# A four-layer decoder trunk on one core: tensor-engine operands that begin at eight different 32-byte offsets within 256 bytes

## The chip, the core and the metric

The kernel runs on one core of one Trainium2 chip. The metric is the device time of one execution in microseconds (us), taken as the median of several runs. Lower is better.

## The reference

The reference is a decoder trunk of four layers over one residual stream of 256 tokens by 1024 features, all in float32. Each layer is a token mixer followed by a squared-ReLU MLP of width 4096. Layers 0 and 3 mix by differential attention, layer 1 by block attention (with 256 tokens there is one block, so it is causal attention), layer 2 by a sliding window of 128 with sinks. Cut to what matters:

```python
for i in range(DEPTH):                       # 4
    a = rms_norm(h, attn_norm_g[i])
    y = mixer(i % 3)(a, w_in, w_out, ...)    # diff, moba, swa, diff
    h = h + y
    a = rms_norm(h, mlp_norm_g[i])
    u = jnp.maximum(a @ w_up[i], 0)          # 1024 -> 4096
    h = h + (u * u) @ w_down[i]              # 4096 -> 1024
return rms_norm(h, final_norm_g)
```

## The kernel before, in words

The residual stream is held transposed in SBUF: features on the 128 partitions, 256 tokens along the free axis, in four tiles `hT`. All weights are streamed once from HBM as pieces of 128 partitions by 2048 floats (8 KB a partition) into `raw` tiles, of which there are four.

Each product keeps near-float32 accuracy by splitting both operands into a rounded part and the rest, both of type float32r ("hi" and "lo"), and adding hi·hi, hi·lo and lo·hi. `stage` (L71 to L82) makes the two parts of each weight piece: ScalarE copies `raw` into `whi` (L80), VectorE writes the difference into `wlo` (L81), three buffers of each. `norm_part` (L220 to L227) makes the two parts of the normalized stream in four tiles `hg`, and `up_proj` (L648 to L668) those of the MLP's hidden activations, `uu`, in the slots below. `take` (L86) hands the next piece to the stage that wants it and keeps the pieces ahead fetched and split.

TensorE's work is a long row of matmuls, each with its own weight load of 128 by 128. In the MLP a `block_step` (L590) issues a pair: the hi weights against the hi and lo parts of the activations side by side (512 moving columns, L591), and the lo weights against the hi part alone (256 columns, L592). The first projections of the mixers (`proj`, L273) and the last down-projection (`down_out`, L679) issue triples, with the weight piece as the moving operand, of 512 columns and in the sliding-window layer of 256; the scores (`scores`, L311) and the differential layers' output projection (`out_proj_all`, L615) issue triples too, through `mm3` (L267).

All that is neither streamed nor constant lives in one SBUF pool, `sb`. Its large tiles share slots by number: `room(j, ...)` (L52) gives a tile in slot j, 0 to 17, and every tile that was in that slot before must be done first. A slot is 4096 bytes a partition. The names in it: `uu` in the MLP; `qk`, `qhl`, `kpadh`, `kpadl`, `v`, `e`, `et`, `oo` in the mixers.

The order of instructions on each engine is set by a scheduler when the program is built: it takes the program order and the tiles' buffers and lets an instruction go ahead when its operands and its buffer are free in its own model. `junk` (L396) is a tile with one buffer into which ScalarE writes squares that nobody reads; only their sums (`ss`) are used, in the differential layers (`diff_pair`, L389).

Of the kernel before, what the change touches and what calls it, by code (L numbers as in the profile page):

```python
# [11 lines left out]
F32 = mybir.dt.float32  # L12
F32R = mybir.dt.float32r
# [5 lines left out]
P = 128  # L19
D = 1024  # L20
S = 256
# [7 lines left out]
LOOK = 2  # L29
FAR = 5  # L30
WARM = 12
RAW = 4


def f(ap):
    return ap.bitcast(F32)
# [3 lines left out]
def trunk(ctx: ExitStack, tc: tile.TileContext, xT, gains, lams, swa_row, fng, weights, out):  # L40
# [5 lines left out]
    sb = ctx.enter_context(tc.tile_pool(name="sb", bufs=2))  # L46
    ps = ctx.enter_context(tc.tile_pool(name="ps", bufs=4, space=bass.MemoryType.PSUM))

    def bank(tag, name):
        return ps.tile([P, 512], F32, tag=tag, name=name, bufs=4)  # L50

    def room(j, shape, name, dt=F32):  # L52

        return sb.tile(shape, dt, tag=f"slot{j}", name=name, bufs=1)


    fetched, staged = [], []
# [1 line left out]
    def fetch(parts=1, first=None):  # L59

        i = len(fetched)
        raw = sb.tile([P, 2048], F32, tag="raw", name=f"raw{i}", bufs=RAW)
        w = 2048 // parts
# [7 lines left out]
    def stage(w=1024, first=None):  # L71
        i = len(staged)
        raw = fetched[i]
        hi = sb.tile([P, 2048], F32R, tag="whi", name=f"whi{i}", bufs=LOOK + 1)
        lo = sb.tile([P, 2048], F32R, tag="wlo", name=f"wlo{i}", bufs=LOOK + 1)
        for h in range(2048 // w):
            if first:
                first()
            s = slice(h * w, (h + 1) * w)
            A.activation(hi[:, s], raw[:, s], AF.Copy)  # L80
            V.tensor_tensor(lo[:, s], raw[:, s], f(hi[:, s]), op=OP.subtract)  # L81
        staged.append((hi, lo))  # L82
# [3 lines left out]
    def take():  # L86
        i = used[0]
        used[0] += 1
        while len(fetched) < min(weights.shape[0], i + FAR + 1):
            fetch()  # L90
        while len(staged) < min(weights.shape[0], i + LOOK + 1):
            stage()
        return staged[i]

    def r3(n):
        return lambda t: t.rearrange("p (a b) -> p a b", a=n)
# [43 lines left out]
    def bcast(dram, n):  # L140
        return bass.AP(tensor=dram.tensor, offset=dram.offset, ap=[[0, P], [1, n]])
# [46 lines left out]
    def lambdas():  # L188
        lam_init = [0.8 - 0.6 * math.exp(-0.3 * i) for i in (0, 3)]
        lv = room(4, [P, 4, 2, HD], "lv")  # L190
        nc.sync.dma_start(lv, bcast(lams, 8 * HD))
        lp = sb.tile([P, 2, 2, HD], F32, tag="ropea", name="lp")
        V.tensor_tensor(lp, lv[:, 0::2], lv[:, 1::2], op=OP.mult)
        ls = cst.tile([P, 2, 2], F32, name="ls")
        V.tensor_reduce(ls, lp, axis=AX.X, op=OP.add)
        A.activation(ls, ls, AF.Exp)
        V.tensor_tensor(nlam, ls[:, 1], ls[:, 0], op=OP.subtract)
        for s in range(2):
            V.tensor_scalar(nlam[:, s:s + 1], nlam[:, s:s + 1], -lam_init[s], None, op0=OP.add)
            V.tensor_scalar(sg[:, s:s + 1], sg[:, s:s + 1], 1.0 - lam_init[s], None, op0=OP.mult)  # L200

    def rsqrt(y, x, n):

        t = tiny.tile([P, n], F32, tag="nw", name="nw", bufs=6)
        V.tensor_scalar(y.bitcast(I32), x.bitcast(I32), -0.5, 1597463007.0, op0=OP.mult, op1=OP.add)
        for _ in range(3):
            V.tensor_tensor(t, y, y, op=OP.mult)
            V.scalar_tensor_tensor(t, t, -0.5, x, op0=OP.mult, op1=OP.mult)
            V.scalar_tensor_tensor(y, t, 1.5, y, op0=OP.add, op1=OP.mult)
# [5 lines left out]
    def new_norm(gain):  # L215
        n = Normed()
        n.gain, n.both, n.acc = gain, [], None
        return n

    def norm_part(n, d):  # L220

        j, b = d // 2, d % 2
        if b == 0:
            n.both.append(sb.tile([P, 2, 2, S], F32R, tag=f"hg{j}", name=f"hg{j}", bufs=1))
        both, h, g = n.both[j][:, b], hT[j][:, S * b:S * b + S], n.gain[:, d:d + 1]
        A.activation(both[:, 0], h, AF.Copy, scale=g)  # L226
        V.scalar_tensor_tensor(both[:, 1], h, g, f(both[:, 0]), op0=OP.mult, op1=OP.subtract)  # L227
# [83 lines left out]
    def scores(q, k, mask, sinks):  # L311
# [8 lines left out]
        out = []  # L320
        scored[0] += 1
        pair_e = room(4 + scored[0] % 2, [P, 2, 3 * P], "e")
        for c in range(2):
            ns = sb.tile([P, 3 * P], F32, tag="ns", name="ns", bufs=2)
# [18 lines left out]
    def transposed(es):  # L343
        turned[0] += 1
        ts = room((6, 7, 12, 13)[turned[0] % 4], [P, 2, 3 * P], "et")
        for i, e in enumerate(es):
            p = bank("wk", "p_t")
            for j in range(3):
                T.transpose(p[:, P * j:P * j + P], e[:, P * j:P * j + P], ident)  # L349
            A.activation(ts[:, i], p[:, :3 * P], AF.Copy)  # L350
        return [ts[:, i] for i in range(len(es))]

    def times_v(o, et, v):

        T.matmul(o(0), et[:, 0:P], v(0), start=True, stop=True)
        T.matmul(o(1), et[:, P:2 * P], v(0), start=True, stop=False)
        T.matmul(o(1), et[:, 2 * P:3 * P], v(1), start=False, stop=True)
# [9 lines left out]
    def part(b, n=1):  # L367

        if b % 2 == 0:
            pair[:] = [room(14 + b // 2, [P, 2, 2, S], "oo", F32R)]  # L370
        return pair[0] if n == 2 else pair[0][:, b % 2]
# [17 lines left out]
    def diff_pair(slot, ets, v, el, b):  # L389

        p = bank("wk", "p_av")
        for c in range(2):
            times_v(lambda t, c=c: p[:, S * c + P * t:S * c + P * t + P], ets[c], v[c])
        ss = tiny.tile([P, 2 * NT], F32, tag="ss", name="ss")
        for t in range(2 * NT):
            junk = sb.tile([P, P], F32, tag="junk", name="junk", bufs=1)  # L396
            A.activation(junk, p[:, P * t:P * t + P], AF.Square, accum_out=ss[:, t:t + 1])
        V.scalar_tensor_tensor(ss, ss, 1.0 / P, el, op0=OP.mult, op1=OP.add)
        y = tiny.tile([P, 2 * NT], F32, tag="ry", name="ry")
        rsqrt(y, ss, 2 * NT)  # L400
        o = sb.tile([P, 2 * NT, P], F32, tag="o", name="o")
        V.tensor_tensor(o, p.rearrange("p (t m) -> p t m", m=P), y[:, :, None].to_broadcast([P, 2 * NT, P]),
                        op=OP.mult)
        yield
        p = bank("wk", "p_o")
        for t in range(2 * NT):
            T.transpose(p[:, P * t:P * t + P], o[:, t, :], ident)
        both, gain = part(b, 2), sg[:, slot:slot + 1]
        A.activation(both[:, :, 0], r3(2)(p), AF.Copy, scale=gain)
        V.scalar_tensor_tensor(both[:, :, 1], r3(2)(p), gain, f(both[:, :, 0]), op0=OP.mult, op1=OP.subtract)  # L410
        yield [both[:, 0], both[:, 1]]
# [61 lines left out]
    def mixer_layer(i, n):  # L473
# [46 lines left out]
        else:  # L520
# [25 lines left out]
            def AV(h):  # L546
                if mixer:
                    next(heads[h], None)
                elif h % 2:
                    pairs[h // 2] = diff_pair(slot, [ets[h - 1], ets[h]], [vh(h - 1), vh(h)], els[h // 2], h - 1)  # L550
                    next(pairs[h // 2])
# [48 lines left out]
    def into(n, d, p, row, whole=False):  # L600

        j, b = d // 2, d % 2
        h = hT[j][:, S * b:S * b + S]
        y = p
        if not whole:
            y = sb.tile([P, S], F32, tag="y", name="y")
            joined(y, p)
        if row is not None:
            V.tensor_tensor(y, y, row, op=OP.mult)
        V.tensor_tensor(h, y, h, op=OP.add)  # L610
        norm_part(n, d)
        if b:
            norm_sum(n, j)
# [65 lines left out]
    def down_out(us, res, factor):  # L679

        grow = sb.tile([P, D], F32, tag="raw", name="grow", bufs=RAW)
        nc.sync.dma_start(grow, bcast(fng, D))
# [31 lines left out]
    n = new_norm(gv[:, 0, 0, :])  # L714
    blocks = iter(range(8))
    for _ in range(2):
        stage(512, lambda: norm_part(n, next(blocks)))
    for j in range(4):
        norm_sum(n, j)
    for i in range(DEPTH):  # L720
        parts = mixer_layer(i, n)
        n = new_norm(gv[:, 1, i, :])
# [24 lines left out]
        if i + 1 < DEPTH:  # L747
            n = new_norm(gv[:, 0, i + 1, :])
# [80 lines left out]
```

## Time and profile before

| what | value |
|---|---|
| median of the runs shown | 1160.81 us (1160.3, 1160.81, 1161.35) |
| profiled execution, first to last instruction (span) | 1158.7 us |
| TensorE matmuls in the trace | 6484, busy 1140.8 us |
| TensorE weight loads, busy | 980.9 us |
| VectorE, busy | 832.8 us |
| ScalarE, busy | 663.7 us |
| HBM traffic | 197 MB, 171 GB/s over the span |

The profiled execution's own time is its span, 1158.7 us; the timed runs lie about 2.1 us above it, which is what stands before the first and after the last instruction and the spread of the runs. Busy time of TensorE counts matmuls whose ends are modelled and that overlap one another, so it says little of how fast they follow each other. That is read from the starts of matmuls in a long row: the time between two of them, divided by the matmuls between.

### The profile page before, as it was taken

The numbers are of one execution on the slowest core, as the hardware profiler recorded it, in microseconds if no ns is written. First come the engines' busy times: TensorE is split into PE (matmuls) and PEld (weight loads), VectorE is DVE, ScalarE is ACT, GpSimd is POOL, SyncE is SP. The second block draws the span as 40 slices with busy tenths as digits, with TensorE's granted clock in tenths as the row PEclk, the third lists the DMA queues.
The fourth block names the chain that finished last, engine by engine and source line by source line (L and its number), as shares of the span: only waits on it lengthen the run. The fifth ranks groups of instructions, "written<-read, shape, count | busy, mean of one in ns | idle before, by whom it ended". The sixth has DMA issues, their size and how long they took to land.

```text
span 1158.7 us, 16976 instructions
## 1 busy us (share of the span) xinstructions
PE 1140.8 (98%) x6484; PEld 980.9 (85%) x6484; DVE 832.8 (72%) x1672; ACT 663.7 (57%) x1213; POOL 11.4 (1%) x39
## 2 busy tenths in 40 slices
PE   9999999999999999999999999999999999999996
PEld 7788888888887788888899688888888889888885
DVE  7887977656676697775669798775567788777453
ACT  6876656544476666654446665654447676655341
POOL 1000000000000000000000000000000000000000
PEclk9999999999999999999999999999999999999998
DMA  9543465555544355555553245555553444554540
GB/s 330 188 145 111 164 203 193 200 185 184 180 146 146 114 178 202 199 182 186 190 213 127 73 146 190 199 193 182 185 198 132 153 151 141 194 194 163 194 169 37
DMA packets 30321, 198.66 MB, mean 171 GB/s; under 512 B 3488, under 2 KB 4640, under 8 KB 7072
## 3 DMA queue, kind: packets, MB, share of 16 engines
q1 hardware_dynamic: 29952, 197.06, 49.3%
q8 instruction: 51, 0.84, 0.3%
q10 hardware_dynamic: 288, 0.52, 0.1%
q14 instruction: 30, 0.25, 0.1%
HBM read 196.52 MB, written 1.05 MB: 171 GB/s over the span
## 4 chain that ended last, share of the span: by engine, by line
PE 89%; DVE 6%; ACT 2%; DMA 1%; issue 1%; SPq 0%; ACTq 0%
PE p_up L591 20%; PE p_in L294 15%; PE p_down L591 15%; PE p_up L592 10%; PE p_down L592 8%; PE p_last L270 2%; PE p_last L269 2%; PE p_last L271 2%; DVE wlo L81 2%; PE p_e L591 1%; PE p_t L349 1%; PE p_d L591 1%; PE p_s L269 1%; DMA raw<-in_weights 1%; PE p_av L429 1%
## 5 line engine op out<-in xcount | busy, mean ns | idle before, releaser
L81 DVE TENSOR_TENSOR wlo<-raw,whi 128x1024 fp32r<-128x1024 f32 (+1 forms) x374 | 447.3, 1209 | 203.3 <-ACT whi L80 202.8
L80 ACT ACTIVATE whi<-raw 128x1024 fp32r<-128x1024 f32 (+1 forms) x374 | 384.2, 1045 | 211.9 <-issue 109.8
L591 PE MATMUL p_up<-hg,whi 128*128 128x512 f32 x1024 | 356.8, 393 | 0.2
L592 PE MATMUL p_up<-hg,wlo 128*128 128x256 f32 x1024 | 285.2, 279 | 0.0
L591 PE MATMUL p_down<-uu,whi 128*128 128x512 f32 x768 | 266.4, 392 | 0.0
L591 PEld LDWEIGHTS p_up<-hg,whi 128*128 128x128 f32 x1024 | 191.6, 187 | 43.3 <-DVE hg L227 0.7
L592 PE MATMUL p_down<-uu,wlo 128*128 128x256 f32 x768 | 214.3, 279 | 0.0
L294 PE MATMUL p_in<-whi,hg 128*128 128x512 f32 (+1 forms) x736 | 212.5, 371 | 0.3 <-ACT whi L80 0.2
L592 PEld LDWEIGHTS p_up<-hg,wlo 128*128 128x128 f32 x1024 | 193.2, 189 | 0.4
L591 PEld LDWEIGHTS p_down<-uu,whi 128*128 128x128 f32 x768 | 143.7, 187 | 32.2
L294 PEld LDWEIGHTS p_in<-whi,hg 128*128 128x128 f32 x736 | 132.1, 188 | 23.5 <-ACT whi L80 1.3
L592 PEld LDWEIGHTS p_down<-uu,wlo 128*128 128x128 f32 x768 | 144.8, 188 | 0.0
L294 PE MATMUL p_in<-wlo,hg 128*128 128x512 f32 (+1 forms) x368 | 129.9, 368 | 0.2 <-DVE wlo L81 0.2
L664 ACT ACTIVATE uu<-u 128x512 fp32r<-128x512 f32 x64 | 40.5, 633 | 72.2 <-DVE u L662 72.2
L294 PEld LDWEIGHTS p_in<-wlo,hg 128*128 128x128 f32 x368 | 68.8, 189 | 11.7 <-DVE wlo L81 0.8
L597 ACT ACTIVATE cross<-p_up 128x256 f32<-128x256 f32 x128 | 48.2, 376 | 39.6 <-PE p_up L592 34.8
L226 ACT ACTIVATE hg<-hT,gn 128x256 fp32r<-128x256 f32 x64 | 31.7, 502 | 66.4 <-DVE hT L610 65.0
L334 ACT ACTIVATE e<-ns,nm 128x128 f32<-128x128 f32 (+1 forms) x128 | 56.9, 446 | 11.0 <-DVE nm L331 10.3
L665 DVE TENSOR_TENSOR uu<-u,uu 128x512 fp32r<-128x512 f32 x64 | 44.2, 691 | 21.8 <-ACT uu L664 21.8
L598 DVE TENSOR_TENSOR relu<-p_up,cross 128x256 f32<-128x256 f32 x128 | 53.5, 418 | 1.4 <-ACT cross L597 1.3
L271 PE MATMUL p_last<-whi,uu 128*128 128x512 f32 x128 | 49.8, 389 | 0.0
L270 PE MATMUL p_last<-wlo,uu 128*128 128x512 f32 x128 | 49.8, 389 | 0.0
(181 smaller groups left out, 1245.1 us busy)
## 6 DMA issues: line engine op xcount, KB each, us to landing
raw<-in_weights SPq DMA_DIRECT2D x181, 1024.0 KB, 4.9
raw<-in_weights SPq DMA_DIRECT2D x8, 256.0 KB, 4.5
raw<-in_weights SPq DMA_DIRECT2D x4, 512.0 KB, 8.1
hT<-in_xT SPq DMA_DIRECT2D x8, 128.0 KB, 4.3
bias<-in_swa_row SPq DMA_DIRECT2D x1, 512.0 KB, 3.5
grow<-in_fng SPq DMA_DIRECT2D x1, 512.0 KB, 3.7
out<-res ACTq DMA_DIRECT2D x2, 256.0 KB, 2.7
out<-res SPq DMA_DIRECT2D x2, 256.0 KB, 2.7
```

The source lines that it names most:

```text
L80: A.activation(hi[:, s], raw[:, s], AF.Copy)
L81: V.tensor_tensor(lo[:, s], raw[:, s], f(hi[:, s]), op=OP.subtract)
L270: T.matmul(out, lh, rl, start=False, stop=False, **kw)
L271: T.matmul(out, ll, rh, start=False, stop=stop, **kw)
L294: T.matmul(out[t], n.both[k // 2][:, k % 2, x, P * t:P * t + P], r3(kb)(parts[k // kb][w])[:, k % kb, :], start=fresh, stop=k == 7 and x + ...
L334: A.activation(e[:, s], ns[:, s], AF.Exp, bias=nm[:, t:t + 1], scale=-1.0, accum_out=l[:, t:t + 1])
L591: T.matmul(r3(2)(p), hi, x, start=start, stop=False, skip_group_check=True)
L592: T.matmul(p[:, :S], lo, x[:, 0], start=False, stop=stop, skip_group_check=True)
L597: A.activation(cross, p[:, S:], AF.Copy)
L598: V.tensor_tensor(out, p[:, :S], cross, op=OP.add)
L664: A.activation(both[:, :, 0], r3(2)(u), AF.Copy)
L665: V.tensor_tensor(both[:, :, 1], r3(2)(u), f(both[:, :, 0]), op=OP.subtract)
```

## The change

The tiles that TensorE reads get 8 floats (32 bytes) more than they need, and only the first part of each is used. Since the pool places tile behind tile, each buffer then begins 32 bytes further on, modulo 256, than the one before it. This is done for the buffers of `whi` and `wlo`, the four `hg` and the slots 0 to 12; the slots 13 to 17 stay at 4096 bytes. To make room, `junk` gives up its own 512 bytes and takes a buffer of `y`, a tile with two buffers.

```diff
+STEP = 8
...
     def room(j, shape, name, dt=F32):
-        return sb.tile(shape, dt, tag=f"slot{j}", name=name, bufs=1)
+        n = math.prod(shape[1:])
+        t = sb.tile([P, 1024 + STEP * (j < 13)], dt, tag=f"slot{j}", name=name, bufs=1)[:, :n]
+        if len(shape) == 2:
+            return t
+        axes = "abcd"[:len(shape) - 1]
+        return t.rearrange(f"p ({' '.join(axes)}) -> p {' '.join(axes)}",
+                           **{a: k for a, k in zip(axes[1:], shape[2:])})
...
-        hi = sb.tile([P, 2048], F32R, tag="whi", name=f"whi{i}", bufs=LOOK + 1)
-        lo = sb.tile([P, 2048], F32R, tag="wlo", name=f"wlo{i}", bufs=LOOK + 1)
+        hi = sb.tile([P, 2048 + STEP], F32R, tag="whi", name=f"whi{i}", bufs=LOOK + 1)[:, :2048]
+        lo = sb.tile([P, 2048 + STEP], F32R, tag="wlo", name=f"wlo{i}", bufs=LOOK + 1)[:, :2048]
...
-            n.both.append(sb.tile([P, 2, 2, S], F32R, tag=f"hg{j}", name=f"hg{j}", bufs=1))
+            t = sb.tile([P, 4 * S + STEP], F32R, tag=f"hg{j}", name=f"hg{j}", bufs=1)
+            n.both.append(t[:, :4 * S].rearrange("p (a b c) -> p a b c", b=2, c=S))
...
-            junk = sb.tile([P, P], F32, tag="junk", name="junk", bufs=1)
+            junk = sb.tile([P, P], F32, tag="y", name="junk")
```

Where the tiles begin, as the built programs have it (byte address in a partition modulo 256, divided by 32, so 0 to 7; buffers or slots in turn):

```
tile                      before      after
raw (4 buffers)           7 7 7 7     7 7 7 7
whi (3 buffers)           7 7 7       7 0 1
wlo (3 buffers)           7 7 7       2 3 4
hg0 to hg3                7 7 7 7     5 6 7 0
kpadh, kpadl, v0, v1      7 7 7 7     1 2 3 4
the other padded slots    7           5 6 7 0 1 2 3 4 5
slots 13 to 17            7           5 6 6 6 6
hT, ident, ones           4 6 6       4 6 6
```

Slices of these tiles begin a multiple of 512 bytes from the tile's start, so a slice has the number of its tile. All 5904 matmuls of type float32r read, before, a moving and a stationary operand with the same number; after, 482 of them do, and each other difference, 1 to 7, has 592 to 866 of them. The pool ends 224 bytes further up.

No instruction is added, taken away or changed in size, but `junk` has two buffers now instead of one, and so the scheduler puts a few instructions in another place in the layers 0 and 3. On ScalarE, in layer 0, at the second pair of heads (`whi_986` is the weight piece split next, `junk` the squares of `p_av`, `e` the exponentials of the next heads' scores) there stood before:

```order
L80 ACTIVATE whi_986<-raw_684 128x1024
L397 ACTIVATE junk,ss<-p_av 128x128
L80 ACTIVATE whi_986<-raw_684 128x1024
L397 ACTIVATE junk,ss<-p_av 128x128
L334 ACTIVATE e,l<-ns,nm 128x128
L397 ACTIVATE junk,ss<-p_av 128x128
L334 ACTIVATE e,l<-ns,nm 128x256
L397 ACTIVATE junk,ss<-p_av 128x128
L334 ACTIVATE e,l<-ns,nm 128x128
L334 ACTIVATE e,l<-ns,nm 128x256
```

On the same engine at the same place there stands now (line numbers here are those of the changed kernel, 7 or 8 higher):

```order
L87 ACTIVATE whi_986<-raw_684 128x1024
L405 ACTIVATE junk,ss<-p_av 128x128 x4
L342 ACTIVATE e,l<-ns,nm 128x128
L87 ACTIVATE whi_986<-raw_684 128x1024
L342 ACTIVATE e,l<-ns,nm 128x256
L342 ACTIVATE e,l<-ns,nm 128x128
L342 ACTIVATE e,l<-ns,nm 128x256
```

The four squares stand in one row, ahead of one half of a weight split and of the exponentials, which they stood between. On TensorE, a little later in layer 0, where the second pair's output `o` is transposed into `p_o` between matmuls of the fifth projection, there stood before:

```order
L454 MATMUL p_qk<-ident,qk 128x128 x8
L294 MATMUL p_in<-whi_796,hg_145 128x512
L294 MATMUL p_in<-wlo_797,hg_145 128x512
L407 MATMUL p_o<-ident,o 128x128 x4
L294 MATMUL p_in<-whi_796,hg_145 128x512 x2
```

On TensorE at the same place there stands now:

```order
L462 MATMUL p_qk<-ident,qk 128x128 x8
L302 MATMUL p_in<-whi_796,hg_145 128x512
L415 MATMUL p_o<-ident,o 128x128 x4
L302 MATMUL p_in<-wlo_797,hg_145 128x512
L302 MATMUL p_in<-whi_796,hg_145 128x512 x2
```

The transposes go one matmul earlier. The same pieces move in layer 3; besides, one or two matmuls of the output projection change places with a `p_o`, twice in each of the two layers. In layers 1 and 2 TensorE's order is the same.

## The prediction

> **What bounds the kernel now.** I began with the profile page's busy times, its chain of work that ended last, and the view of the cores for the granted clock.
>
> ```profile
> span 1158.7 us, 16976 instructions
> PE 1140.8 (98%) x6484; PEld 980.9 (85%) x6484; DVE 832.8 (72%) x1672; ACT 663.7 (57%) x1213; POOL 11.4 (1%) x39
> PE 89%; DVE 6%; ACT 2%; DMA 1%; issue 1%; SPq 0%; ACTq 0%
> core 0: 1158.7 us, clock 0.997
> ```
>
> TensorE has work in 98% of the span, 89% of the chain lies on it, and its clock is granted in full. So the time is that of a row of matmuls, and the question is what one matmul costs. The groups by line and shape show which ones count:
>
> ```profile
> L591 PE MATMUL p_up<-hg,whi 128*128 128x512 f32 x1024 | 356.8, 393 | 0.2
> L592 PE MATMUL p_up<-hg,wlo 128*128 128x256 f32 x1024 | 285.2, 279 | 0.0
> L591 PE MATMUL p_down<-uu,whi 128*128 128x512 f32 x768 | 266.4, 392 | 0.0
> L592 PE MATMUL p_down<-uu,wlo 128*128 128x256 f32 x768 | 214.3, 279 | 0.0
> L294 PE MATMUL p_in<-whi,hg 128*128 128x512 f32 x576 | 182.5, 395 | 0.3 <-ACT whi L80 0.2
> L294 PE MATMUL p_in<-wlo,hg 128*128 128x512 f32 x288 | 108.4, 390 | 0.2 <-DVE wlo L81 0.2
> L271 PE MATMUL p_last<-whi,uu 128*128 128x512 f32 x128 | 49.8, 389 | 0.0
> ```
>
> The means (393 ns, 279 ns) overlap one another, so they are not what a matmul costs. That comes from first and last starts in long rows: of the first layer's down-projection (each of these with an L592 behind it), of the last stage (each with an L270 and an L271 behind it), and, in the timeline, of an output projection of 256 columns, where the rows from 112.93 to 118.33 us hold 16 starts of L269, each again with two more behind it:
>
> ```profile
> L591 PE MATMUL p_down<-uu,whi x256: 391/391/391, 212.9 to 301.3; 128*128 128x512 f32 x128
> L269 PE MATMUL p_last<-whi,uu x121: 389/389/389, 1064.2 to 1145.8; 128*128 128x512 f32 x121
> 112.93 0.28 PE L269 MATMUL p_d<-oo,whi 128*128 128x256 f32 x1
> ...
> 118.33 0.28 PE L269 MATMUL p_d<-oo,whi 128*128 128x256 f32 x1
> ```
>
> A pair of 512 and 256 columns takes (301.3 − 212.9) / 255 = 346.7 ns, a matmul of 512 takes (1145.8 − 1064.2) / 120 / 3 = 226.7 ns, one of 256 takes (118.33 − 112.93) / 15 / 3 = 120.0 ns. From the last two, a column costs (226.7 − 120.0) / 256 = 0.417 ns and each matmul 226.7 − 512 × 0.417 = 13.3 ns on top, whatever its width; and the pair confirms it: 768 × 0.417 + 2 × 13.3 = 346.7. The program holds 5904 float32r matmuls, 3264 of 512 columns and 2640 of 256: 3264 × 226.7 + 2640 × 120.0 = 1056.7 us of the span's 1158.7. Of that, 5904 × 13.3 = 78.7 us is the 13.3 ns. Each of these matmuls has its own weight load beside it, so the 13.3 ns may be a fixed price of a matmul with a new weight, or the price of two streams that read SBUF at once and meet. Only in the second case can start addresses matter.
>
> **The change part by part.** The first part is the addresses. Before, all 5904 have both operands at the same offset modulo 256; after, 5422 have them at different ones. No row of before shows a float32r matmul with different offsets, so I bound it by the nearest rows: float32 ones, some of which have.
>
> ```profile
> L355 PE MATMUL p_av<-v,et 128*128 128x128 f32 x32 | 6.2, 275 | 0.0
> L454 PE MATMUL p_qk<-ident,qk 128*128 128x128 f32 x96 | 12.7, 273 | 1.2 <-DVE qk L307 1.2
> L741 PE MATMUL p_res<-ident,hT 128*128 128x128 f32 x16 | 1.9, 272 | 0.0
> ```
>
> In p_av the two operands have the same offset (275 ns), in p_qk they are 32 bytes apart (273 ns), in p_res 64 bytes (272 ns). The first is a product and the others are transposes, but the three stand within 3 ns, where 13.3 would show. Also, the 13.3 ns is the same at 256 columns as at 512, and in the down-projection all 256 matmuls have 391 ns at minimum, median and maximum, while `uu` runs through 16 slots and ScalarE, VectorE and DMA come and go beside them. Two streams that met by chance would scatter. A fixed price explains this with the least, so I take 0. The bounds: −78.7 us if all of it were meetings and none were left, and on the other side what the rows show as the slower beat of the same pair, in the stage p_e:
>
> ```profile
> 410.10 0.40 PE L591 MATMUL p_e<-oo,whi 128*128 128x512 f32 x1
> 410.33 0.28 PE L592 MATMUL p_e<-oo,wlo 128*128 128x256 f32 x1
> ...
> 412.57 0.40 PE L591 MATMUL p_e<-oo,whi 128*128 128x512 f32 x1
> L591 PE MATMUL p_e<-oo,whi 128*128 128x512 f32 x64 | 22.8, 400 | 0.0
> ```
>
> Seven pairs here take 2.47 us, 352.9 ns each, 6.2 more than in the down-projection, at the same offsets and in the same shapes. So there is a second beat that widths and offsets do not explain; on all 1920 pairs (1024 + 768 + 64 + 64) it would cost +11.9 us.
>
> A rule of the Trainium skill speaks against any effect: "TensorE: Matmul & The Clock Gate", section "Step-by-step: what each phase is for", says that TensorE has two independent read ports into SBUF, one for the moving operand and one for weight loads, so that loading the next weights takes no bandwidth from the running matmul. By it this part is exactly 0 and the lower bound of −78.7 us falls away; that the extra is the same at both widths agrees with it, and no run here shows a float32r matmul with different offsets yet. The same page of the Trainium skill, section "Wait — 56ns, not 53.3ns?", speaks the other way: it gives columns / 2.4 GHz + about 2.5 ns from matmul to matmul, 215.7 ns for 512. The trace has the same slope but 226.7 ns; by the Trainium skill 11 ns of the 13.3 would be avoidable, an estimate of 5904 × 11 = 65 us.
>
> The second part is ScalarE and VectorE, whose operands get other offsets too. The nearest rows with equal and with different offsets:
>
> ```profile
> L609 DVE TENSOR_TENSOR y<-y,row 128x256 f32<-128x256 f32 x24 | 10.1, 419 | 0.0
> L610 DVE TENSOR_TENSOR hT<-y,hT 128x256 f32<-128x256 f32 x40 | 16.9, 424 | 1.1
> L81 DVE TENSOR_TENSOR wlo<-raw,whi 128x1024 fp32r<-128x1024 f32 (+1 forms) x374 | 447.3, 1209 | 203.3 <-ACT whi L80 202.8
> ```
>
> `y` and `row` have the same offset, `y` and `hT` are 96 bytes apart: 419 against 424 ns. Five ns on each of the 374 weight splits would be 1.9 us of VectorE, which is idle for 28% of the span and waits 203 us ahead of this very line: covered, 0. Without that cover it would cost those 1.9 us.
>
> The third part is what the scheduler moved. Squares of `p_av` go ahead of a weight split and exponentials in layers 0 and 3; so `o` is done earlier and the transposes `p_o` wait less.
>
> ```profile
> PE p_o L407 <- DVE o L402: 2.4, 6, 0.5
> PEld p_o L407 <- issue: 2.5, 4, 0.7
> 78.55 0.27 ACT L397 ACTIVATE junk<-p_av 128x128 f32<-128x128 f32 x1
> ...
> 81.12 0.28 ACT L397 ACTIVATE junk<-p_av 128x128 f32<-128x128 f32 x1
> 81.28 0.21 ACT L397 ACTIVATION_READ_ACCUMULATOR junk<-p_av 128x1 f32 x1
> 86.09 0.63 PE L407 MATMUL p_o<-ident,o 128*128 128x128 f32 x4 [0.31 <-DVE o L402]
> ```
>
> The four squares ran from 78.55 to 81.49 us; in one row they need about 4 × 0.25 = 1.0, so they end nearly 2 us sooner. TensorE stood still for 2.4 us in all ahead of `p_o`, in six places, 0.4 us each. Six of the eight `p_o` move up, each by a single matmul of 0.12 to 0.23 us, so I take a third of it, −0.8 us. What is behind them pays: the `whi` half and the exponentials on ScalarE, and who waits for those (`wlo` on VectorE, the transposes p_t on TensorE), start up to 1 us later, and a `p_o` that is now one matmul earlier waits in front of that matmul if `o` is late. Bounds −2.4 and +2.4 us. No DMA and no queue of SyncE or GpSimd is passed. `junk` in a buffer of `y` waits for `y`'s last reader, which is the MLP of the layer before, long done.
>
> The sum: 1158.7 − 0.8 = 1157.9 us for the span, and with the 2.1 us by which the median of the runs (1160.8) stands above that span, 1160.0 us.
>
> **The rivals.** First, the weight loads do meet the moving stream, and equal offsets are the bad case. For it: an extra per matmul that no other row explains. Against: it does not scatter, and the float32 rows at three distances agree. Removing half of it gives −39 us, 1121 us; all of it 1081 us.
>
> Second, only the slower beat goes, because it is a matter of how the two streams start against each other. By the group means, p_in has 395 and 390 ns against 389 in the last stage (576 × 6 + 288 × 1 = 3.7 us), p_up 393 against 391 (1024 × 2 = 2.0 us), p_e 400 against 391 (64 × 9 = 0.6 us): −6.3 us together, 1153.7 us with the reorder. For it: two beats at one shape exist. Against: the offsets are equal in both, so something else chooses.
>
> Third, and on the other side, different offsets put the pairs into the slower beat: up to +11.9 us, 1172 us. It decides from 2.3 / 0.0062 = 370 pairs of 1920 on. For it: the beat exists and is stable over a whole stage. Against: the same as above.
>
> Fourth, the change doesn't do what it says: the addresses in the built program say it does, for 92% of the matmuls.
>
> **How the numbers follow.** A measurement of this kernel can tell about 0.2% (2.3 us) from no change. No effect of the addresses and the reorder within its bounds: 0.53. The first rival 0.15, the second 0.14, the third 0.18; the fourth would end in the first case and gets nothing. The likeliest gives 1160.0. Faster is the first two rivals, 0.29; the same 0.53; slower 0.18. Leaving out the first rival alone leaves 0.85, so the range goes from the second rival with the reorder's lower bound, 1160.8 − 6.3 − 2.4 = 1152, to the third with its upper bound, 1160.8 + 11.9 + 2.4 = 1175. The likeliest case's own range is 1158.4 to 1163.2.
>
> **What would show it.** If I am right, the starts of the down-projection's pairs stay 346.7 ns apart and the last stage's matmuls 226.7, in every slot, and `p_o` waits a little less. The first rival would show a pair below 340 ns, and pairs that differ with the slot of `uu`. The third would show 353 ns where 346.7 stood. VectorE's 1209 ns at L81 should stay within 10 ns. I am wrong if any pair of long rows moves by more than 1.2 ns, which is 2.3 us over 1920 pairs.

## The result and the profile after

The changed kernel takes 1168.29 us (median of 4 runs, 1167.56 to 1169.09) against 1160.55 for the kernel before (4 runs, 1159.66 to 1161.35): a ratio of 1.0066, 95% interval 1.0051 to 1.0080. It is slower by 7.7 us, where no change was forecast, and on the side of the third rival.

The page of the changed kernel (the profiled execution took 1169.1 us):

```profile
span 1167.1 us, 16974 instructions
PE 1151.1 (99%) x6484; PEld 983.7 (84%) x6484; DVE 831.5 (71%) x1672; ACT 663.7 (57%) x1213; POOL 11.4 (1%) x39
PE 90%; DVE 5%; ACT 2%; DMA 1%; issue 1%; SPq 0%; ACTq 0%
L88 DVE TENSOR_TENSOR wlo<-raw,whi 128x1024 fp32r<-128x1024 f32 (+1 forms) x374 | 447.1, 1209 | 213.2 <-ACT whi L87 212.8
```

The span grew by 8.4 us and TensorE's busy time by 10.3, with the same 6484 matmuls; the other engines are where they were, VectorE's weight split at 1209 ns as before, with 10 us more of waiting ahead of it. (The page counts two instructions fewer than before, 16974 for 16976: semaphore instructions of VectorE, which the moves alone take away too, as the first experiment's page shows.) So the matmuls themselves are slower. The groups by line and shape say which:

```profile
L599 PE MATMUL p_up<-hg,whi 128*128 128x512 f32 x1024 | 360.7, 396 | 0.3 <-DVE hg L235 0.2
L600 PE MATMUL p_up<-hg,wlo 128*128 128x256 f32 x1024 | 286.3, 280 | 0.0
L599 PE MATMUL p_down<-uu,whi 128*128 128x512 f32 x768 | 269.0, 394 | 0.0
L600 PE MATMUL p_down<-uu,wlo 128*128 128x256 f32 x768 | 215.1, 280 | 0.0
L302 PE MATMUL p_in<-whi,hg 128*128 128x512 f32 x576 | 184.7, 399 | 0.4 <-ACT whi L87 0.4
L277 PE MATMUL p_last<-whi,uu 128*128 128x512 f32 x128 | 50.4, 394 | 0.0
```

The four 512-column groups in these lines are up by 2 to 5 ns (393, 392, 395 and 389 before); a smaller one, `p_e`, went down, from 400 to 395 ns. As before, what a matmul costs comes from first and last starts. The view of one line of the changed kernel, in the first layer's down-projection and in the last stage:

```profile
L599 PE MATMUL p_down<-uu,whi x256: 388/394/401, 213.9 to 303.2; 128*128 128x512 f32 x128
L277 PE MATMUL p_last<-whi,uu x128: 387/394/400, 1068.7 to 1156.9; 128*128 128x512 f32 x128
```

A pair now takes (303.2 − 213.9) / 255 = 350.2 ns instead of 346.7, and a matmul of the last stage (1156.9 − 1068.7) / 127 / 3 = 231.5 instead of 226.7. The three durations, 391/391/391 before, now run from 388 to 401: the matmuls differ with the buffers they read.

Worked out from the starts of all matmuls: the time from one start to the next, less the columns at 0.417 ns and less 13.3 ns, added up by tile. Steps that are more than 100 ns longer than that hold a wait or other work and are left out:

```
us beyond      p_up  p_down  p_in  p_last  p_d   p_s   p_e
before         0.70  0.00    4.39  0.04    2.11  3.13  0.42
after          4.61  2.64    7.08  1.83    1.52  2.95  0.12
```

In all that is +10.0 us. Ahead of `p_o`, on the other hand, TensorE waits less, as the waits of the changed kernel show (2.4 us before):

```profile
PE p_o L415 <- DVE o L410: 0.6, 2, 0.3
```

10.0 − 1.8 = 8.2 us of the span's 8.4.

### The profile page after: what moved, and what is told of

Read it like the earlier page. It is cut to its first block, busy times and chain, and to the rows that moved or that the text cites. A ratio compares the mean times of both kernels' runs of the same rounds, so it can differ in the third digit from the quotient of the medians.

```text
span 1167.1 us, 16974 instructions
## 1 busy us (share of the span) xinstructions
PE 1151.1 (99%) x6484; PEld 983.7 (84%) x6484; DVE 831.5 (71%) x1672; ACT 663.7 (57%) x1213; POOL 11.4 (1%) x39
## 4 chain that ended last, share of the span: by engine, by line
PE 90%; DVE 5%; ACT 2%; DMA 1%; issue 1%; SPq 0%; ACTq 0%
PE p_up L599 20%; PE p_in L302 16%; PE p_down L599 15%; PE p_up L600 10%; PE p_down L600 8%; PE p_last L277 2%; PE p_last L279 2%; PE p_last L278 2%; DVE wlo L88 2%; PE p_e L599 1%; PE p_t L357 1%; PE p_d L599 1%; PE p_s L277 1%; PE p_qk L462 1%; DMA raw<-in_weights 1%
## 5 line engine op out<-in xcount | busy, mean ns | idle before, releaser
L88 DVE TENSOR_TENSOR wlo<-raw,whi 128x1024 fp32r<-128x1024 f32 (+1 forms) x374 | 447.1, 1209 | 213.2 <-ACT whi L87 212.8
L599 PE MATMUL p_up<-hg,whi 128*128 128x512 f32 x1024 | 360.7, 396 | 0.3 <-DVE hg L235 0.2
L342 ACT ACTIVATE e<-ns,nm 128x128 f32<-128x128 f32 (+1 forms) x128 | 56.9, 448 | 11.0 <-DVE nm L339 10.3
L277 PE MATMUL p_last<-whi,uu 128*128 128x512 f32 x128 | 50.4, 394 | 0.0
L279 PE MATMUL p_last<-whi,uu 128*128 128x512 f32 x128 | 50.3, 393 | 0.0
```

The costliest lines, as they stand in the source:

```text
L277: T.matmul(out, lh, rh, start=start, stop=False, **kw)
L279: T.matmul(out, ll, rh, start=False, stop=stop, **kw)
L342: A.activation(e[:, s], ns[:, s], AF.Exp, bias=nm[:, t:t + 1], scale=-1.0, accum_out=l[:, t:t + 1])
L599: T.matmul(r3(2)(p), hi, x, start=start, stop=False, skip_group_check=True)
```

## The experiments

My theory after the result: the distance, modulo 256 bytes, between the operand that is streaming and the weights that are loaded beside it sets how long a matmul takes, and distance 0 happens to be a good one for these shapes. The rivals: it is the offset of a tile as such, whatever the other operand's; it is only a distance that changes from matmul to matmul; it is the scheduler's moves; it is other engines or DMAs, whose accesses fall differently now.

**The moves alone.** The kernel before with one edit, so that all addresses of TensorE's operands stay equal modulo 256:

```diff
-            junk = sb.tile([P, P], F32, tag="junk", name="junk", bufs=1)
+            junk = sb.tile([P, P], F32, tag="y", name="junk")
```

> The kernel before with junk in a buffer of y alone: the scheduler's moves without any other start address. If the start addresses made the changed kernel slower, this one lies within 0.2% of the kernel before, 1158 to 1163 us, and its down-projection pairs stay 346.7 ns apart. If the moved instructions did it, it lies near 1168 us with pairs still at 346.7 ns.

1159.25 us, ratio 0.9988 (0.9979 to 0.9998). Its page, the down-projection's line and the wait ahead of `p_o`:

```profile
span 1156.2 us, 16974 instructions
L591 PE MATMUL p_down<-uu,whi x256: 391/391/391, 211.7 to 300.1; 128*128 128x512 f32 x128
PE p_o L407 <- DVE o L402: 0.5, 2, 0.3
```

The pair stays at 346.7 ns. The moves gain 1.3 us, mostly through `p_o`. So the addresses cost about 9 us, the difference of the two.

**All offsets shifted, no distance changed.** 32 bytes ahead of the whole pool, so that every operand begins at 0 instead of 224 modulo 256:

```diff
+    cst.tile([P, 8], F32, name="shift")
```

> The kernel before with every tile of the pool 32 bytes further on, so that all float32r operands begin at 0 instead of 224 modulo 256, and still all at the same offset. If the distance between the two operands counts, nothing changes: 1158 to 1163 us, pairs 346.7 ns. If the offset itself counts (224 is a good one), it is slower, by about as much as the changed kernel: 1165 to 1171 us.

1160.82 us, ratio 1.0001 (0.9991 to 1.0011). The same line:

```profile
L593 PE MATMUL p_down<-uu,whi x256: 391/391/391, 213.4 to 301.8; 128*128 128x512 f32 x128
```

Again 346.7 ns. A step of 32 bytes that all operands make together does nothing; other common steps were not tried.

**One distance for all.** A tile of 128 bytes ahead of the first `hg`, so that the activations lie 128 bytes from both halves of the weights, always:

```diff
+            if not made:
+                made.append(sb.tile([P, 32], F32, tag="gap", name="gap", bufs=1))
```

> The kernel before with one gap of 128 bytes between the weight tiles and everything behind them: the weights and the activations are 128 bytes apart in nearly every matmul, always the same distance. If a distance other than 0 is dear in itself, the pairs go to 350 ns or more and the time to 1167 us or above. If only a distance that changes from matmul to matmul is dear, this is as before, 1158 to 1163 us.

1171.01 us, ratio 1.0094 (1.0078 to 1.0109). The same line and the last stage's:

```profile
L595 PE MATMUL p_down<-uu,whi x256: 387/396/398, 213.7 to 303.2; 128*128 128x512 f32 x128
L273 PE MATMUL p_last<-whi,uu x128: 390/393/404, 1070.5 to 1159.1; 128*128 128x512 f32 x128
```

A pair takes 351.0 ns and a matmul of the last stage 232.5. One distance, nothing spread, the program order of before: this is the whole loss and a little more. Of the rivals the last is left, other engines and DMAs.

**Bare rows of matmuls.** Five kernels hold nothing but a copy of some data and long rows of float32r matmuls on it; they do not compute the reference, and each ran once. The first runs pairs of 512 and 256 columns at all 64 combinations of the hi and the lo weights' distance from the moving operand, in steps of 32 bytes, 24 pairs each:

```diff
+                T.matmul(p, wh[:, 256 * k + 8 * a:256 * k + 8 * a + P], mv[:, m:m + 512], start=k == 0,
+                T.matmul(p[:, :S], wl[:, 256 * k + 8 * b:256 * k + 8 * b + P], mv[:, m:m + S], start=False,
```

> Not the reference's computation: a bare row of matmul pairs (512 and 256 moving columns, each with its own weights) for all 64 combinations of the two weight operands' distances from the moving one, 0 to 224 bytes in steps of 32, 24 pairs each, with no other engine at work. If distances count, the combination 0 and 0 takes 346.7 ns a pair and others 340 to 355, each with a value of its own. If it is other engines' traffic, or change from matmul to matmul, that made the pairs slower, all 64 settle at 346.7.

Worked out from the starts, ns per pair, from the ninth pair of each combination on (the first eight of the very first row take 640 to 807 ns each):

```
hi \ lo     0     32     64     96    128    160    192    224
   0      347.4  346.2  346.6  346.7  346.7  346.7  351.1  352.9
  32      351.5  353.8  348.7  350.0  353.7  350.7  351.1  346.5
  64      340.0  347.1  353.3  353.5  349.6  346.7  353.3  351.1
  96      346.7  352.0  353.5  346.7  351.1  353.3  348.0  353.3
 128      352.0  351.1  346.7  351.4  351.1  351.1  346.7  346.7
 160      349.3  346.7  348.9  353.5  346.7  350.1  353.3  346.7
 192      350.0  346.7  346.7  348.9  346.7  349.3  353.3  348.9
 224      344.5  348.9  346.5  346.7  348.9  353.3  353.3  346.7
```

With no other engine at work, and nothing on the DMA queues beside the copies in and out but 0.39 MB that the page lists as kind "instruction", the pair still moves between 340.0 and 353.8 ns with nothing but the addresses: the last rival is not needed. The mean of the table is 349.4; the kernel's tiles, spread over all eight, came to 350.2. Before sat at (0, 0), one of the good places.

The second runs matmuls of one width, 512 and then 256 columns, at distances from 0 to 632 bytes in steps of 8:

> Not the reference's computation: a bare row of single matmuls of 512 and then of 256 moving columns, with the weights 0 to 632 bytes from the moving operand in steps of 8, 24 matmuls at each. If two read streams meet in parts of the memory that repeat every 256 bytes, the times repeat after 32 steps and have steps as wide as such a part. If each matmul has a fixed price with its weight load, all stand at 226.7 and 120.0 ns, and only pairs of unequal widths feel distances.

The view of its line in four windows, each within one distance: 256 and 320 bytes with 512 columns, 512 and 576 bytes with 256 columns:

```profile
L42 PE MATMUL p<-mv,wh x20: 389/389/393, 203.8 to 208.1; 128*128 128x512 f32 x20
L42 PE MATMUL p<-mv,wh x20: 393/396/398, 248.3 to 252.8; 128*128 128x512 f32 x20
...
L42 PE MATMUL p<-mv,wh x19: 279/283/283, 652.8 to 654.9; 128*128 128x256 f32 x19
L42 PE MATMUL p<-mv,wh x20: 276/276/282, 675.5 to 677.7; 128*128 128x256 f32 x20
```

The durations differ; the starts are printed to 0.1 us here, too coarse for 20 short steps. By the starts to the nanosecond, with 512 columns a matmul takes 226.7 ns at distance 0 and at 120 bytes and 228 to 234 at the others, 233.3 at about half of them; with 256 columns 120.0 at 0, 113.3 at 64 and 88 bytes, up to 122 at 24. (Distance 0 with 512 columns is read at 256 and 512 bytes: the very first matmuls, at 0 itself, start 427 ns apart and more.) Apart from that row, distances d, d + 256 and d + 512 give the same times within the reading. So 0 is the best place for the wide matmul and a poor one for the narrow.

In the long rows of the traces a weight load starts 2 to 5 ns after the start of the matmul ahead of its own, so the weights that are loaded beside the narrow matmul are those of the next wide one. A pair may therefore gain where only the wide matmul's weights, the hi part, lie elsewhere: 226.7 + 113.3 = 340.0 ns with the hi part at 64 or 88 bytes and the lo part at 0. The times of single matmuls do not always add up in this way: (64, 64) would come to 233.3 + 113.3 = 346.6, and has 353.3 in the table.

The third is the first in steps of 16 bytes, 256 combinations of 20 pairs:

> Not the reference's computation: the bare pairs of the first row of pairs again, with both distances in steps of 16 bytes, 256 combinations of 20 pairs. If distances act in parts of 32 bytes, neighbours within 32 bytes agree and the least is again 340.0 ns at 64 and 0 bytes. If it is finer, values below 340 may turn up.

340.0 ns at (64, 144), (64, 240) and (192, 16), nothing below it. But (64, 0), at 340.0 in the first, takes 350 here, with other rows ahead of it.

**The best cell, in the kernel.** The table's best cell put into the kernel: `whi` 64 bytes further on, `wlo` and the activations where they were.

```diff
+        if not staged:
+            sb.tile([P, 16], F32, tag="gap64", name="gap64", bufs=1)
         hi = sb.tile([P, 2048], F32R, tag="whi", name=f"whi{i}", bufs=LOOK + 1)
+        if not staged:
+            sb.tile([P, 48], F32, tag="gap192", name="gap192", bufs=1)
```

> The kernel before with the whi buffers alone moved on by 64 bytes, wlo and all else where they were: the best combination of the row of pairs, 340.0 ns. If a bare row's value holds in the kernel, 1920 pairs gain 6.7 ns each, 12.8 us, and the time is near 1148 us, less what the triples with whi as moving operand give or take (up to 4 us). If the distance only disturbs a rhythm that is best when all are equal, it is slower than before, 1163 to 1171 us.

1171.52 us, ratio 1.0094 (1.0077 to 1.0111): a clear miss. The line in the first and in the third layer:

```profile
L595 PE MATMUL p_down<-uu,whi x256: 395/396/396, 215.4 to 305.5; 128*128 128x512 f32 x128
L595 PE MATMUL p_down<-uu,whi x256: 393/394/396, 774.9 to 864.2; 128*128 128x512 f32 x128
```

353.3 and 350.2 ns, where the first bare kernel had 340.0 and the third 350, all at the same distances. The distance alone does not fix the time.

**What else.** The fourth bare kernel takes single widths again and loads 128, 96, 64 or 32 columns of weights:

> Not the reference's computation: a bare row of single matmuls of 512 and of 256 moving columns, whose weight loads have 128, 96, 64 and 32 columns, at distances 0 to 224 bytes, 24 each. If the time on top of the columns is a fixed price of a matmul that brings its own weights, it stays at 13.3 ns for every width of the load at distance 0. If it is made of meetings of the load with the moving stream, it falls with the load's length: about 6.7 ns or less at 64 columns, near 0 to 3 ns at 32.

At distance 0, 256 moving columns have 13.3, 9.5, 6.7 and 6.7 ns on top; 512 have 16.6, 17 and 18.4 with 96, 64 and 32 (and 13.3 with 128, from the second kernel). If the extra were meetings of the two streams one by one, a quarter of the load would leave a quarter of it; if it were a fixed price, it would not move. Neither fits.

The fifth bare kernel runs eleven combinations, each entered in eight ways: after 0 to 7 matmuls of 128 columns.

> Not the reference's computation: bare pairs at eleven combinations of the two distances (0 and 0, 64 and 0, 64 and 120, 88 and 0, 88 and 120, 64 and 144, 64 and 240, 192 and 16, 128 and 128, 64 and 64, 32 and 96 bytes), 32 pairs each, each entered eight times after 0 to 7 matmuls of 128 columns. If a combination's time belongs to its distances alone, the eight entries agree. If several rhythms are stable at the same distances and the entry chooses, they differ by steps of 6.7 ns: 340.0, 346.7, 353.3.

The view of its line in two windows, both at (0, 0), after three and after four such matmuls:

```profile
L48 PE MATMUL p<-mv,wh x28: 395/398/403, 59.8 to 69.4; 128*128 128x512 f32 x28
L48 PE MATMUL p<-mv,wh x27: 391/391/391, 71.9 to 80.9; 128*128 128x512 f32 x27
```

The first is 9.6 / 27 = 0.356 us a pair, the second 9.0 / 26 = 0.346; 353.5 and 346.7 by the starts. At the same addresses a row of pairs falls into one of several rhythms and keeps it over the row's 32 pairs, and how it was entered chooses. (64, 0) has 340.0 in two of its eight entries and 349.9 to 353.5 in six. Some distances have one rhythm only: (88, 0) has 340.0 in all eight, (64, 64) 353.3 in all eight, (128, 128) 351.0 to 351.3. That gives two predictions for the kernel, one each way.

**88 bytes for `whi`.** The moves of the first experiment, and `whi` begins 22 floats further on, the others at 0:

```diff
-        hi = sb.tile([P, 2048], F32R, tag="whi", name=f"whi{i}", bufs=LOOK + 1)
+        hi = sb.tile([P, 2112], F32R, tag="whi", name=f"whi{i}", bufs=LOOK + 1)[:, 22:2070]
```

> The kernel before with junk in a buffer of y and every whi part 88 bytes further on than all other operands (wlo at distance 0). In the bare row this combination took 340.0 ns a pair at all eight entries. If that carries over, 1920 pairs gain 6.7 ns each (12.8 us), two thirds of the output projection's triples gain 6.7 ns (256 of them, 1.7 us), the moved squares give 1.3 us, and the triples with whi as moving operand lose 6.7 ns (832 of them, 5.5 us): about 1150 us. If in the kernel any distance other than 0 leads to a mix of rhythms, 1165 to 1172 us.

1150.34 us, ratio 0.9912 (0.9897 to 0.9927). The down-projection's line and the last stage's:

```profile
L591 PE MATMUL p_down<-uu,whi x256: 388/389/390, 209.9 to 296.6; 128*128 128x512 f32 x128
L269 PE MATMUL p_last<-whi,uu x128: 392/396/399, 1049.3 to 1138.1; 128*128 128x512 f32 x128
```

(296.6 − 209.9) / 255 = 340.0 ns a pair, as the bare row had; but the last stage, where `whi` is the moving operand of triples, goes from 226.7 to 233.1.

**88 bytes only where `whi` is stationary.** The same tile and the same moves, with 22 or 0 floats ahead by the piece's role:

```diff
+        still += [False] * (5 if i % 3 == 2 else 12) + [True] * 20 + [i + 1 < DEPTH] * 16
...
+        at = 22 if still[i] else 0
+        hi = sb.tile([P, 2112], F32R, tag="whi", name=f"whi{i}", bufs=LOOK + 1)[:, at:at + 2048]
```

> The same, but a piece's whi part is 88 bytes further on only where it is the stationary operand (output projections, up and down projections but the last), and at distance 0 where it is the moving one. If distances set the time as in the bare rows, the 5.5 us of the triples stay away: about 1145 us. If distances that differ from stage to stage do harm in themselves, it is no faster than the kernel with 88 bytes everywhere.

1146.30 us, ratio 0.9876 (0.9862 to 0.9891): the fastest, ahead of both kernels. Its page and the two lines:

```profile
span 1144.8 us, 16974 instructions
L595 PE MATMUL p_down<-uu,whi x256: 388/389/390, 211.2 to 297.9; 128*128 128x512 f32 x128
L273 PE MATMUL p_last<-whi,uu x128: 388/389/395, 1048.2 to 1134.6; 128*128 128x512 f32 x128
```

340.0 ns a pair and (1134.6 − 1048.2) / 127 / 3 = 226.8 a matmul of the last stage. 1920 pairs × 6.7 ns = 12.8 us and the moves' 1.3 make 14.1 us, and 14.0 were gained (1160.27 us for the kernel before in the same series). The 1.7 us that the output projection's triples were to add are not seen whole: `p_d`, with its 64 pairs, falls by 1.0 us in the sum by tile.

**64 bytes for both halves.** The other way: `whi` and `wlo` 64 bytes on, the activations at 0, the program order of before.

```diff
+        if not staged:
+            sb.tile([P, 16], F32, tag="gap64", name="gap64", bufs=1)
...
+            if not made:
+                made.append(sb.tile([P, 48], F32, tag="gap192", name="gap192", bufs=1))
```

> The kernel before with whi and wlo both 64 bytes further on than the operands they meet. In the bare row 64 and 64 took 353.3 ns a pair at all eight entries. If that carries over, 1920 pairs lose 6.3 ns against 347.0 (12.1 us), triples of 512 columns lose 2.2 ns (1248, 2.7 us) and those of 256 gain (3.0 us): about 1172 us. If a bare row's times do not hold in the kernel, it lies elsewhere, near 1160 us if a single distance for both parts does no harm.

1172.58 us, ratio 1.0105 (1.0088 to 1.0122):

```profile
L597 PE MATMUL p_down<-uu,whi x256: 397/398/398, 214.0 to 304.1; 128*128 128x512 f32 x128
```

90.1 / 255 = 353.3 ns, as the bare row said.

What is shown: the distance modulo 256 bytes between the streaming operand and the weights loaded beside it sets the possible rhythms of TensorE's row; where a distance had one rhythm in the bare row, the kernel's pairs took the bare row's time, both ways (340.0, 351 and 353.3 ns). What stays open is what in the chip meets: the extra is not in proportion to the columns loaded, several rhythms are stable at one distance and no rule was found for which entry leads to which, and a float32r matmul without a weight load beside it was not tried.

## Why the prediction was wrong

**The step that failed** is "A fixed price explains this with the least, so I take 0", for the address part: it measured +9 us. Three reasons carried it, and each gave way.

The first was the nearest rows: float32 at equal offsets, 32 and 64 bytes apart, within 3 ns. Those are means of busy time, which the prediction had set aside a paragraph earlier as not what a matmul costs, and of rows of another type and of 128 columns. They could not have shown this. In the changed kernel, where the float32r matmuls are slower, they are what they were:

```profile
L462 PE MATMUL p_qk<-ident,qk 128*128 128x128 f32 x96 | 12.7, 273 | 0.9 <-DVE qk L315 0.9
L364 PE MATMUL p_av<-v,et 128*128 128x128 f32 x32 | 6.2, 275 | 0.0
L749 PE MATMUL p_res<-ident,hT 128*128 128x128 f32 x16 | 1.9, 272 | 0.0
```

The second was that 13.3 ns is the same at both widths. That is so at distance 0, and within 1 ns at 120 bytes, but not in general: at 64 bytes 512 columns have 233.3 − 213.3 = 20.0 ns on top and 256 columns 113.3 − 106.7 = 6.7.

The third was "Two streams that met by chance would scatter". They do not meet by chance. One engine issues both, and the row locks into a rhythm: with 64 bytes the slow pair, too, shows 397/398/398. An even row says that nothing random acts on it, and not that it has no price for meeting.

**The rule of the Trainium skill** that gave exactly 0 ("TensorE: Matmul & The Clock Gate", section "Step-by-step: what each phase is for": two read ports, so the next weights take nothing from the running matmul) does not hold for the time of a matmul here: 226.7 against 233.3 ns for the same matmul with only the weights' address changed. Whether it is at the read ports that something meets, no run here shows. The floor that the same page of the Trainium skill gives in "Wait — 56ns, not 53.3ns?", columns / 2.4 GHz + about 2.5 ns, was not reached by any row here: the least were 226.7 ns for 512 columns and 113.3 for 256.

**The third rival** was the right mechanism: different offsets put the pairs into a slower beat, past its 370 pairs. Its bound was 11.9 us for all pairs at 352.9 ns; `p_up` and `p_down` took 3.91 + 2.64 = 6.6 us more, 3.8 and 3.4 ns a pair instead of 6.2, since the spread mixes good and bad combinations. What it left out are the triples: `p_in` and `p_last` add 2.69 + 1.79 = 4.5 us.

**The second rival** asked what, at equal offsets, chooses between 346.7 and the 352.9 of `p_e`. The bare row at (0, 0) shows it: the entry, 346.7 or 353.5. The kernel shows the same. In layer 2, where the first experiment changes neither an operand's offset modulo 256 nor TensorE's order, `p_e` without its first pair ran before and then, with the moves of layer 0, as

```profile
L591 PE MATMUL p_e<-oo,whi x31: 393/398/403, 667.7 to 678.3; 128*128 128x512 f32 x31
L591 PE MATMUL p_e<-oo,whi x31: 392/395/395, 666.4 to 676.8; 128*128 128x512 f32 x31
```

(678.3 − 667.7) / 30 = 353.3 ns a pair and (676.8 − 666.4) / 30 = 346.7. In the changed kernel `p_e` gains 0.3 us; `p_in` and `p_up`, the rest of that rival's sum, lose. **The first rival**, that meetings are the price and equal offsets the bad case, fails in size and in sign: of the pair's 26.7 ns on top the best distances take away 6.7, and 39 of the 64 in the table add to it.

**The moves** were right in sign and near in size: −0.8 us forecast, −1.3 measured. `p_o` lost 1.8 of its 2.4 us of waiting, more than the third that I took; of the 1.9 us less in the first experiment, 1.3 reached the time. **VectorE and ScalarE** at 0 were right, 1209 ns before and after.

The sign that would show me wrong was well chosen: "if any pair of long rows moves by more than 1.2 ns". It moved by 3.5.

## What to carry to other kernels

Where a kernel is a row of matmuls with a weight load each, measure the time from start to start against the distance of the two operands modulo 256 bytes, in a bare row of the kernel's own shapes and type (here only float32r with 512 and 256 columns was measured), and from several entries; then place the tiles at a distance that has one fast rhythm only, by the role of each tile. Spreading buffers over all offsets gives about the mean of the table, and that is a loss where the start was a good cell. Bound an unknown cost by rows measured in the same way as the cost itself, and do not take an even rhythm for proof that nothing interferes.

## What the runs showed of the hardware

- A float32r matmul of 512 columns with its own weight load takes 226.7 ns at distances 0 and 120 bytes and 228 to 234 at the others; one of 256 columns between 113.3 (64 and 88 bytes) and about 122 (24 bytes). The pattern repeats every 256 bytes.
- A pair of 512 and 256 columns falls into steady rhythms of 340.0, 346.7 or 353.3 ns, 6.7 ns apart, and into mixes of them. At one distance several are stable, and the matmuls ahead choose: at (0, 0) 346.7 or 353.5.
- At distance 0, with 32 columns of weights instead of 128, the extra falls for 256 moving columns (13.3 to 6.7 ns) and rises for 512 (13.3 to 18.4).
- The operands' distance moves this kernel from 1146.3 us (1.3 of the gain is the moves') to 1172.6 us, with the same matmuls.
